# Sparse 3x3 convolution, float32 in and out: the last pair's load in two halves of 32 rows, the second one pair later

## Chip, cores, metric

One core of one Trainium2 chip. The metric is device microseconds (us) of one launch; the profile's span runs from the first to the last instruction and is some 1.8 us shorter. Executions come in a fast and, now and then, in a slow state some per cent longer; the kernel before was caught in it as well (128.5 to 131.5 us in five of its runs).

## The reference

```python
batch, c_in, h, w, c_out, k = 16, 64, 64, 64, 128, 3     # weight: 90% zeros
# x: (16, 64, 64, 64) float32, weight: (128, 64, 3, 3) float32
x_pad = np.pad(x, ((0, 0), (0, 0), (1, 1), (1, 1)))
output[b, co] += weight[co, ci, kh, kw] * x_pad[b, ci, kh:kh+h, kw:kw+w]   # over ci, kh, kw
```

16.8 MB of input are read and 33.55 MB of output are written, both float32 in HBM.

## The kernel before

Images are taken in 8 pairs: two images of 64 channels fill the 128 partitions. A GpSimd DMA loads each pair and casts it to bf16. Each pair has four blocks of 16 rows. For a block GpSimd adds neighbouring rows (tile `s`), TensorE runs 30 matmuls, ScalarE copies a shared product, and VectorE adds it to the two others into the output buffers `o`. The SP queue stores them. All pairs' inputs have a buffer of their own; outputs have seven buffers, two for a pair.

```python
xs = [x_pool.tile([128, H, W], BF16, name=f"x{p}") for p in range(NP)]      # NP = 8
...
def load(p, a=0, b=H):
    nc.gpsimd.dma_start(out=xs[p][:, a:b, :], in_=pair(p)[:, a:b, :])

EARLY, CUT = 4, 24
for p in range(1, EARLY):
    load(p)
load(EARLY, 0, CUT)
...                                        # weights are transposed; product(), direct(), twos()
for p in range(NP):
    o = [o_pool.tile([C_OUT, H, W], FP32, name="o") for _ in range(2)]
    last = p == NP - 1
    for blk in range(4):
        r0 = 16 * blk
        if BLOCKS[p][blk] == "T":
            twos(p, o, r0)                 # GpSimd add, matmuls, ScalarE copies, VectorE adds
            if p == 1 and blk == 3:
                load(EARLY, CUT, H)
            elif p > 1 and blk == 3 and p + EARLY - 1 < NP:
                load(p + EARLY - 1)        # pair 5 after pair 2, 6 after 3, 7 after 4
        ...
        if last and blk % 2 == 1:
            for n in range(2):
                rows = slice(r0 - 16, r0 + 16)
                nc.sync.dma_start(out=out[2 * p + n][:, rows, :], in_=o[n][:, rows, :])
    if not last:
        for n in range(2):
            nc.sync.dma_start(out=out[2 * p + n], in_=o[n])
```

## Time and profile before

| | before |
|---|---|
| median of the first three runs | 126.33 us (126.23 to 126.84) |
| span of the profiled run | 124.3 us |
| TensorE busy | 108.9 us (88%) |
| VectorE, ScalarE, GpSimd busy | 82.2, 39.0, 41.1 us |
| HBM read and written | 17.07 and 33.55 MB |
| last VectorE add ends / last store packet ends | 112.0 / 123.0 us |

How to read it: an engine's busy share is an average over stages, and the DMA engines are not among the engines of the first table. Read the strip of 40 slices by column: while the DMA row shows 9 in every slice, it hardly matters how full the others are. The queues q0 (loads issued by GpSimd, with cast) and q1 (SP: stores, weights and the first half pair) run on the same 16 DMA engines. The GB/s of the page count a casting load by the bf16 that it writes, half of what it reads; rates that I call HBM rates count loads twice. How long loads take to land is in the page's table of DMA issues (KB by the bf16 side, us from issue to landing):

```profile
x<-in_x_dram POOLq DMA_DIRECT2D x6, 1024.0 KB, 15.7
```

### The profile page before, as it was taken

How to read it: one execution, taken by the hardware profiler on the slowest of the kernel's cores; microseconds unless marked ns; L12 is line 12 of the kernel's file. 1: busy time of each engine (PE TensorE's matmuls, PEld its weight loads, DVE VectorE, ACT ScalarE, POOL GpSimd, SP SyncE). 2: the span in 40 equal slices, each digit the busy share in tenths (PEclk: the TensorE clock that was granted, in tenths of full speed). 3: DMA queues.
4: the chain of work that ended last, by engine and by line, in shares of the span. 5: the costliest groups of instructions: out<-in, count | busy, mean ns of one | idle time of the engine just before them, and what ended most of it. 6: DMA issues, size and time to landing. Idle time of an engine off the chain costs nothing.

```text
span 124.3 us, 2549 instructions
## 1 busy us (share of the span) xinstructions
PE 108.9 (88%) x1030; PEld 59.8 (48%) x1030; DVE 82.2 (66%) x135; ACT 39.0 (31%) x71; POOL 41.1 (33%) x46
## 2 busy tenths in 40 slices
PE   6989999999999999999999999999999999960000
PEld 6845555555555555555555555555555555520000
DVE  0354677877787778777877787778888788870000
ACT  4545323333333333333333333333333333310000
POOL 6428253533353335333533333343333310000000
PEclk9999999999999999999999999999999999998555
DMA  4999999999999999999999999999999999999991
GB/s 130 348 225 216 214 219 213 203 418 311 346 409 411 316 298 327 432 319 329 308 422 332 308 306 409 432 432 430 427 438 416 438 427 432 422 419 414 424 409 82
DMA packets 4196, 42.93 MB, mean 345 GB/s; under 512 B 472, under 2 KB 472, under 8 KB 984
## 3 DMA queue, kind: packets, MB, share of 16 engines
q1 hardware_dynamic: 2888, 34.90, 66.8%
q0 software_dynamic: 1296, 7.86, 30.8%
q8 instruction: 8, 0.13, 0.4%
q14 instruction: 4, 0.03, 0.1%
HBM read 17.07 MB, written 33.55 MB: 407 GB/s over the span
## 4 chain that ended last, share of the span: by engine, by line
PE 82%; DMA 5%; DVE 1%; issue 1%; DVEq 0%; SPq 0%
PE ps L148 82%; DMA o<-in_x_dram 5%; DVE o L181 1%; DVEq L240 0%; DVE x L99 0%; SPq L60 0%; DVEq L181 0%
## 5 line engine op out<-in xcount | busy, mean ns | idle before, releaser
L181 DVE TENSOR_TENSOR o<-ps,pc 128x512 f32<-128x512 f32 x124 | 77.7, 685 | 22.2 <-PE ps L148 19.8
L148 PE MATMUL ps<-x,wT 64*128 64x504 bf16 (+3 forms) x780 | 88.8, 373 | 0.6 <-DVE x L99 0.6
L148 PEld LDWEIGHTS <-wT 64*128 64x128 bf16 x966 | 54.8, 94 | 48.9 <-issue 0.6
L167 POOL TENSOR_TENSOR s<-x 128x512 bf16<-128x512 bf16 x31 | 35.5, 1149 | 57.6 <-PE ps L148 40.2
L174 ACT COPY pc<-ps 128x512 f32<-128x512 f32 x62 | 33.3, 590 | 64.0 <-issue 61.8
L148 PE MATMUL ps<-s,wT 64*128 64x512 bf16 (+1 forms) x186 | 25.7, 377 | 0.0
L84 PE MATMUL ps<-idle_rhs 128*128 128x128 bf16 x55 | 4.8, 265 | 1.0 <-DVE idle_rhs L79 1.0
L84 PEld LDWEIGHTS <-idle_rhs 128*128 128x128 bf16 x55 | 4.4, 122 | 1.0 <-DVE idle_rhs L79 1.0
L68 POOL DMA_DIRECT2D x<-in_x_dram x8 | 4.4, 559 | 0.0
L103 DVE CAST w_bf<-w_sb 128x192 bf16<-128x192 f32 (+1 forms) x4 | 1.1, 345 | 2.7 <-DMA w_sb<-in_weight_dram 2.7
L162 DVE COPY o<-ps 128x512 f32<-128x512 f32 x2 | 1.4, 692 | 2.0 <-PE ps L148 2.0
L161 ACT COPY o<-ps 128x512 f32<-128x512 f32 x2 | 1.2, 586 | 2.4 <-PE ps L148 2.4
L99 ACT CAST x<-o 128x576 bf16<-128x576 f32 (+1 forms) x2 | 1.5, 802 | 1.1 <-DMA o<-in_x_dram 1.1
L99 DVE CAST x<-o 128x576 bf16<-128x576 f32 x1 | 0.5, 459 | 2.1 <-DMA o<-in_x_dram 2.1
L103 ACT ACT_TABLE_LOAD x1 | 1.3, 1283 | 0.7 <-PEq L229 0.7
L103 ACT CAST w_bf<-w_sb 128x64 bf16<-128x64 f32 (+1 forms) x2 | 0.7, 416 | 1.6 <-DMA w_sb<-in_weight_dram 1.6
L109 PE MATMUL ps<-ident,w_bf 128*128 128x128 bf16 x9 | 1.0, 276 | 0.1
L113 DVE TENSOR_TENSOR wT<-ps,wT 128x384 bf16<-128x384 f32 x2 | 1.0, 546 | 0.0
L109 PEld LDWEIGHTS <-w_bf 128*128 128x128 bf16 x9 | 0.7, 120 | 0.5 <-DVE w_bf L103 0.5
L63 POOL DMA_DIRECT2D x<-in_x_dram x1 | 0.7, 693 | 0.8 <-POOLq L229 0.8
L79 DVE MEMSET idle_rhs<- 128x64 uint32 x1 | 0.1, 112 | 0.8 <-PEq L229 0.8
L122 ACT CAST wT<-ps 128x384 bf16<-128x384 f32 x1 | 0.5, 478 | 0.4 <-PE ps L109 0.4
(8 smaller groups left out, 1.9 us busy)
## 6 DMA issues: line engine op xcount, KB each, us to landing
out_dram<-o SPq DMA_DIRECT2D x14, 2048.0 KB, 17.9
x<-in_x_dram POOLq DMA_DIRECT2D x6, 1024.0 KB, 15.7
out_dram<-o SPq DMA_DIRECT2D x4, 1024.0 KB, 12.0
o<-in_x_dram SPq DMA_DIRECT2D x1, 1024.0 KB
x<-in_x_dram POOLq DMA_DIRECT2D x1, 640.0 KB, 14.3
x<-in_x_dram POOLq DMA_DIRECT2D x1, 512.0 KB, 7.6
x<-in_x_dram POOLq DMA_DIRECT2D x1, 384.0 KB, 25.2
w_sb<-in_weight_dram SPq DMA_DIRECT2D x1, 288.0 KB
```

What stands on the lines that cost most here:

```text
L68: nc.gpsimd.dma_start(out=xs[p][:, a:b, :], in_=pair(p)[:, a:b, :])
L84: nc.tensor.matmul(idle_ps, idle_rhs, idle_rhs, start=True, stop=True)
L99: copy(out=xs[0][:, a:b, :], in_=x_head[:, a:b, :])
L103: copy(out=w_bf4[:, g, a:b, :], in_=w_v[:, k : k + b - a, :])
L109: nc.tensor.matmul(wps[:, j, :], src, ident, start=True, stop=True)
L113: nc.vector.tensor_tensor(out=wT[:, g], in0=wps, in1=wT[:, G1], op=SUB)
L148: nc.tensor.matmul(ps[n][:, lo:hi, c_lo:c_hi], tap(g, kw, n), src[q, a:b:step, c_lo + kw - 1 : c_hi + kw - 1], start=(i == 0), stop=(i == ...
L161: nc.scalar.copy(out=o[0][:, r0 : r0 + rows, :], in_=ps[0])
L162: nc.vector.tensor_copy(out=o[1][:, r0 : r0 + rows, :], in_=ps[1])
L167: nc.gpsimd.tensor_tensor(out=s, in0=xs[p][:, r0 : r0 + 16 : 2, :], in1=xs[p][:, r0 + 1 : r0 + 16 : 2, :], op=ADD)
L174: nc.scalar.copy(out=c, in_=shared[n])
L181: nc.vector.tensor_tensor(out=o[n][:, first : r0 + 16 : 2, :], in0=ps[n], in1=pc[n], op=ADD)
```

## The change

The intent: make room for stores where the last load stood, and let its second half come one pair later.

```diff
     EARLY, CUT = 4, 24
+
+    LATER = {2: (5,), 3: (6,), 4: (7, 0, 32), 5: (7, 32, 64)}
     for p in range(1, EARLY):
         load(p)
     load(EARLY, 0, CUT)
@@
                 if p == 1 and blk == 3:
                     load(EARLY, CUT, H)
-                elif p > 1 and blk == 3 and p + EARLY - 1 < NP:
-                    load(p + EARLY - 1)
+                elif blk == 3 and p in LATER:
+                    load(*LATER[p])
```

## The prediction

> **What bounds the kernel now.** I read the page's strip of 40 slices first, then its DMA lines, then the chain of waits, then windows of the late part, and last the GpSimd timeline, because the change moves a GpSimd load. From the page:
>
> ```profile
> span 124.3 us, 2549 instructions
> PE   6989999999999999999999999999999999960000
> DMA  4999999999999999999999999999999999999991
> ...
> q1 hardware_dynamic: 2888, 34.90, 66.8%
> q0 software_dynamic: 1296, 7.86, 30.8%
> ...
> HBM read 17.07 MB, written 33.55 MB: 407 GB/s over the span
> ```
>
> TensorE is full until slice 36 and then has nothing to do for the last tenth of the span, while the DMA row is at 9 from slice 2 to slice 39. The two queues (q1 stores, q0 the casting loads) together take 66.8 + 30.8 = 97.6% of the 16 engines' time. The loads count half in the GB/s row, as that counts the bf16 that is written; by HBM bytes it is 17.07 + 33.55 = 50.62 MB. The chain of waits, in order of time, ends earlier than the program does:
>
> ```profile
> 7.38 102.09 PE ps L148 x954
> ...
> 111.42 0.60 DVE o L181
> ```
>
> It follows TensorE for 102 us and stops at 112.02 us, where the last VectorE add ends. The other 12.3 us are the stores draining, which this view does not follow. Windows show the late part (columns: us, busy time of PE, PEld, DVE, ACT, POOL with counts, granted clock, DMA share, GB/s):
>
> ```profile
> 76.00:80.00 4.00, 4.00 (x42) 2.06 (x38) 3.22 (x6) 1.72 (x4) 1.33 (x2) 1.00 1.03 438
> 80.00:84.00 4.00, 4.00 (x40) 2.13 (x38) 2.59 (x5) 1.50 (x3) 2.13 (x2) 1.00 0.98 416
> 84.00:88.00 4.00, 4.00 (x42) 2.15 (x38) 3.41 (x6) 1.07 (x2) 1.15 (x1) 1.00 1.01 430
> ...
> 112.00:116.00 4.00, 0.00 (x0) 0.00 (x0) 0.02 (x1) 0.00 (x0) 0.00 (x0) 0.76 1.00 422
> 116.00:120.00 4.00, 0.00 (x0) 0.00 (x0) 0.00 (x0) 0.00 (x0) 0.00 (x0) 0.50 1.01 428
> 120.00:121.00 1.00, 0.00 (x0) 0.00 (x0) 0.00 (x0) 0.00 (x0) 0.00 (x0) 0.50 0.93 393
> 121.00:122.00 1.00, 0.00 (x0) 0.00 (x0) 0.00 (x0) 0.00 (x0) 0.00 (x0) 0.50 0.60 254
> 122.00:123.00 1.00, 0.00 (x0) 0.00 (x0) 0.00 (x0) 0.00 (x0) 0.00 (x0) 0.50 0.16 66
> ```
>
> The reader is to see that stores alone run at about 428 GB/s (mean of 438, 416, 430) with a DMA share of 1, that this goes on after the compute has ended, and that only the last 2 to 3 us taper off, as the 16 engines do not finish together. 50.62 MB / 428 GB/s = 118.3 us of pure transfer inside a span of 124.3; what remains is the first few us, the taper and the final completion. So the bound is the total of DMA bytes. TensorE comes close behind it: in the drain window (112 to 124.3) 4.11 MB still move, of which the last two stores, issued at 111.45 and 112.04, are 2.10 MB. So 2.0 MB, 4.7 us at 428 GB/s, were already queued ahead of them: TensorE could end some 4.7 us later before the DMA engines ran dry.
>
> **What the Trainium skill says.** "DMA: Bandwidth & Descriptors", section "Issuing engines are not separate DMA queues", says that DMAs from any issuing engine end up on the same 16 DMA engines and interleave. The trace agrees: while load and stores overlap, from 62 to 77 us, the queue shares are 34.8% and 66.5%, 101% in sum. The same page, section "Where 436 GB/s comes from", gives 435 GB/s as the ceiling of a core's SBUF ports; it also says that HBM binds at about 358 GB/s. The trace agrees with the first (428 in steady state) and not with the second, so I use 428. The same page, section "Queues, rings and completion order", says each DMA engine goes round robin between its queues by packets. The trace agrees in kind: a load beside queued stores lands after 15.7 us (median), where 2.1 MB of HBM alone would take 4.9 us.
>
> **The change, part by part.** It leaves pairs 5 and 6 (loads at the ends of pairs 2 and 3) as they are. The load of pair 7, one issue of 64 rows after the last block of pair 4, becomes 32 rows there and 32 rows after the last block of pair 5. GpSimd's timeline of before gives the moments:
>
> ```profile
> 60.25 1.15 POOL L167 TENSOR_TENSOR s<-x 128x512 bf16<-128x512 bf16 x1 [2.01 <-PE ps L148]
> 61.34 0.57 POOL L68 DMA_DIRECT2D x<-in_x_dram  x1
> ...
> 73.05 1.15 POOL L167 TENSOR_TENSOR s<-x 128x512 bf16<-128x512 bf16 x1 [2.01 <-PE ps L148]
> 76.20 1.15 POOL L167 TENSOR_TENSOR s<-x 128x512 bf16<-128x512 bf16 x1 [2.00 <-issue]
> ...
> 95.50 1.16 POOL L167 TENSOR_TENSOR s<-x 128x512 bf16<-128x512 bf16 x1 [2.09 <-PE ps L148]
> 98.67 1.15 POOL L167 TENSOR_TENSOR s<-x 128x512 bf16<-128x512 bf16 x1 [2.01 <-PE ps L148]
> ```
>
> Counting four adds to a pair back from the last, 98.67 is the last block of pair 7, 73.05 that of pair 5 and 60.25 that of pair 4.
>
> 1. Bytes: none added, none removed. The 1.05 MB (HBM side) of the second half go from 61 to 77 us to the stretch after 74 us. Both stretches are full, so the stores take over what is freed, 1.05 MB / 428 = 2.5 us earlier at most, and give it back in the second stretch. Effect on the end: 0.
> 2. GpSimd: one more issue of 0.56 us (the median of the eight), at about 74.1, in an idle stretch of 2.0 us before the add at 76.20. Off the path: 0.
> 3. Packets: 128 more data packets and 16 more 4-byte ones, as a load has 144 packets (1296 in nine loads). In the DMA records of the trace a load packet that reads 16 KB takes 0.624 us and one that reads 8 KB 0.324: two halves are 0.024 us dearer. 128 pairs x 0.024 / 16 engines = 0.19 us, and 16 x 0.02 / 16 = 0.02 us: +0.21. The store packets give less: 0.309 for 8 KB against 0.611 for 16 KB, 0.007 a pair, so 8 x 0.007 = 0.06 us. The 8 KB load packets ran beside the start's other loads, which flatters the difference, so I take +0.1 us.
> 4. Deadline of the second half. Each engine has eight load packets. In before these eight 16 KB packets, beside stores, took from about 62 to 76 us: 14 us, or 1.75 us a turn, of which 0.62 is the load packet and about 1.1 are stores. With 8 KB packets a turn is 1.1 + 0.32 = 1.45 us, and eight are 11.6 us; with 1.5 us of issue and completion the half lands at about 74.1 + 13 = 87. GpSimd first reads it for the third block of pair 7, at 95.50: 8 us in hand. TensorE reads row 32 in the odd rows of the second block, at about 102.9 by its timeline. Nobody waits: 0.
>
> Sum: 126.33 + 0.1 = 126.4 us.
>
> **The rivals.**
>
> *A: the second half lands late and stalls TensorE.* For it: a load has taken up to 25.2 us to land (the one at the start, queued behind the others); 25 us from 74.1 is 99.3, after the add at 95.50. Against it: beside stores the loads took 14.3 to 15.7 us, and this is half of one. Even at 99.3 the add would have to be done only before TensorE wants its result at 104.08 (the third block of pair 7), and an end of TensorE up to 4.7 us later is still hidden by the queued stores. Time if it came true in this form: 126.4 to 126.9. To cost 2% (2.5 us) the stall would have to pass 7 us.
>
> *B: the stores that go earlier free an output buffer sooner, and the kernel gains.* There are seven output buffers for two per pair, so the second output of pair 6 reuses that of the first store of pair 3, which landed at 79.5, some 6 us before pair 6 writes. That is the tightest I find. But no wait of VectorE on an output store is in the list of waits:
>
> ```profile
> DVE o L181 <- PE ps L148: 19.8, 27, 1.3
> DVE o L181 <- ACT pc L174: 2.3, 4, 0.6
> ```
>
> These are the only waits of the add: the matmuls and the ScalarE copy. A buffer freed sooner releases nobody. Gain: 0.
>
> *C: the stores run dry for a moment because the load has left their stretch, and the DMA engines idle.* By 73 us five pairs' outputs, 21 MB, are about to be queued and the stores' queue has moved some 13.3 MB, so over 7 MB wait, 17 us of work; taking 1.05 MB from this leaves over 6 MB. Cost: 0.
>
> *D: the order of packets changes how unevenly the engines finish.* The taper from 120 to 123 us moves (0.93 + 0.60 + 0.16) = 1.7 us worth of full work in 3 us, so 1.3 us are lost to unevenness. I can't tell from the profile which engine is late or why. If the change shifts it, it is by some tenths either way: 126.0 to 126.8.
>
> **Range and chances.** The centre is 126.4. The three runs before already span 126.23 to 126.84, so the noise is about 0.6; D adds some tenths either way, A and the packet cost only upward. Range for 8 in 10: 125.9 to 127.0. Faster by over 2% means under 123.8, which is less than the present end of transfers allows: everything lost at both ends is about 124.3 - 118.3 = 6 us, and the change touches none of it; chance 0.02. Slower by over 2% means above 128.9, which needs A far beyond any landing seen, or a loss in mixing the queues that no stretch of before shows; chance 0.03. Within 2%: 0.95.
>
> **What would show it right or wrong.** Right: the strip's DMA row at 9 as before; q0 with 1440 packets and the same 7.86 MB; one more load issue near 74 us; half loads landing 11 to 15 us after issue; no GpSimd wait on a load after the first 20 us; windows at 420 to 438 GB/s from 88 us; the last add at 112 us; the span within 0.5 us of 124.3. Step 4 is wrong if the list of waits shows adds or matmuls waiting for the load of pair 7 after 90 us, and step 1 is wrong if a window between 61 and 90 us has a DMA share well below 1. A taper shorter or longer than 3 us with all else equal would be D. A time below 124 or above 129 would mean that the DMA bound itself is misread.

## The result

126.31 us median against 126.31 us, six runs each. The ratio of the fast runs is 0.9988, with a 95% interval of 0.9965 to 1.001: the same time. (A ratio is the mean time of one kernel's fast runs over that of the other's fast runs in the same rounds, so it is not quite the ratio of the medians.) One of the six runs of the changed kernel was slow, 131.61 us. Such runs came with the kernel before too, so nothing is read from it.

The page of the changed kernel, the lines that answer to those of before:

```profile
span 124.2 us, 2550 instructions
...
DMA  4999999999999999999999999999999999999992
...
q1 hardware_dynamic: 2888, 34.90, 67.0%
q0 software_dynamic: 1440, 7.86, 30.9%
...
x<-in_x_dram POOLq DMA_DIRECT2D x3, 512.0 KB, 13.7
```

One instruction and 144 packets more, the same bytes, the same full DMA row. (Three loads are of 512 KB: the two halves of pair 7 and the half of pair 0 at the start.) The chain of waits still ends with the last VectorE add at 112.1 us, while the stores run on:

```profile
7.51 102.04 PE ps L150 x954
...
111.49 0.60 DVE o L183
```

GpSimd's timeline has the new issue where it was expected, and no add of pair 7 comes late:

```profile
73.12 1.15 POOL L169 TENSOR_TENSOR s<-x 128x512 bf16<-128x512 bf16 x1 [2.01 <-PE ps L150]
74.22 0.57 POOL L68 DMA_DIRECT2D x<-in_x_dram  x1
76.29 1.14 POOL L169 TENSOR_TENSOR s<-x 128x512 bf16<-128x512 bf16 x1 [1.50 <-issue]
...
95.56 1.15 POOL L169 TENSOR_TENSOR s<-x 128x512 bf16<-128x512 bf16 x1 [2.08 <-issue]
```

What did move is the order of the bytes. In windows of the changed kernel (same columns as before) the GB/s of 72 to 76 us is 417 where it was 342, because half a load is gone from there and stores have its place; from 80 to 88 us it is the other way round (416 and 430 before, in the prediction; 357 and 389 now). First the line of before, then those of the changed kernel:

```profile
72.00:76.00 4.00, 4.00 (x42) 2.16 (x38) 3.41 (x6) 1.08 (x2) 1.15 (x1) 1.00 1.00 342
```

```profile
72.00:76.00 4.00, 4.00 (x42) 1.86 (x40) 3.42 (x6) 1.07 (x2) 1.66 (x2) 1.00 1.02 417
...
80.00:84.00 4.00, 4.00 (x40) 1.82 (x38) 2.55 (x6) 1.57 (x4) 1.83 (x2) 1.00 1.05 357
84.00:88.00 4.00, 4.00 (x42) 1.89 (x40) 3.41 (x6) 1.07 (x2) 1.15 (x1) 1.00 1.00 389
...
120.00:121.00 1.00, 0.00 (x0) 0.00 (x0) 0.00 (x0) 0.00 (x0) 0.00 (x0) 0.50 0.97 410
```

The DMA share, second from the right, is 0.97 or more in each of these. The first store of pair 3 landed at 76.8 us instead of 79.5, so the stores do run 2.7 us ahead for a while, and by the last ones nothing of it is left: the first of the last four landed at 115.9 against 116.1, and the last packet ended at 122.9 against 123.0.

### The profile page after: what moved, and what is told of

Same layout as the page of the kernel before. It is cut to its first block, busy times and chain, and to the rows that moved or that the text cites. A ratio compares the mean times of both kernels' runs of the same rounds, so it can differ in the third digit from the quotient of the medians.

```text
span 124.2 us, 2550 instructions
## 1 busy us (share of the span) xinstructions
PE 109.7 (88%) x1030; PEld 52.9 (43%) x1030; DVE 82.2 (66%) x135; ACT 38.9 (31%) x71; POOL 41.6 (34%) x47
## 4 chain that ended last, share of the span: by engine, by line
PE 85%; DMA 2%; DVE 1%; issue 1%; DVEq 0%
PE ps L150 82%; DMA w_sb<-in_weight_dram 2%; PE ps L86 2%; DVE o L183 1%; PE ps L111 1%; DVEq L242 0%; DVE w_bf L105 0%; DVEq L183 0%
## 5 line engine op out<-in xcount | busy, mean ns | idle before, releaser
L150 PEld LDWEIGHTS <-wT 64*128 64x128 bf16 x966 | 47.1, 94 | 55.8
L150 PE MATMUL ps<-s,wT 64*128 64x512 bf16 (+1 forms) x186 | 25.2, 377 | 0.0
L86 PE MATMUL ps<-idle_rhs 128*128 128x128 bf16 x55 | 5.4, 287 | 1.0 <-DVE idle_rhs L81 1.0
L86 PEld LDWEIGHTS <-idle_rhs 128*128 128x128 bf16 x55 | 5.1, 136 | 1.0 <-DVE idle_rhs L81 1.0
L68 POOL DMA_DIRECT2D x<-in_x_dram x9 | 5.0, 560 | 0.0
L63 POOL DMA_DIRECT2D x<-in_x_dram x1 | 0.7, 693 | 0.8 <-POOLq L231 0.8
```

Of the source, the lines that this page charges most:

```text
L86: nc.tensor.matmul(idle_ps, idle_rhs, idle_rhs, start=True, stop=True)
L150: nc.tensor.matmul(ps[n][:, lo:hi, c_lo:c_hi], tap(g, kw, n), src[q, a:b:step, c_lo + kw - 1 : c_hi + kw - 1], start=(i == 0), stop=(i == ...
```

## Experiments

The theory: the end is set by the total of DMA bytes, at about 428 GB/s of HBM traffic with no gap; TensorE runs a little ahead of that bound, so the order of loads matters only where it makes the DMA engines idle. The rivals: the compute sets the end; loads among the stores cost something of their own; each packet costs something of its own. Eleven kernels, all of them variants of the changed one, were run. Two of them compute wrong results on purpose. Each ratio is to the kernel before, run in the same rounds, which takes the same time as the changed one. The medians are of all runs, the ratios of the fast ones alone; one run each of the kernels without pair 7's load, with quarters and with short packets was slow. A trace is of one execution, the times are of four to six.

### The split alone

```diff
-    LATER = {2: (5,), 3: (6,), 4: (7, 0, 32), 5: (7, 32, 64)}
+    LATER = {2: [(5,)], 3: [(6,)], 4: [(7, 0, 32), (7, 32, 64)]}
-                    load(*LATER[p])
+                    for piece in LATER[p]:
+                        load(*piece)
```

> The split alone: both halves of pair 7's load are issued after the last block of pair 4. Theory (the total of DMA bytes sets the end, and neither packet count nor order of loads matters at this size): same time as before, 126.3, within 0.3 us; both halves land by about 78 us. Rival (each load packet costs a fixed 0.024 us of engine time, 8 more data packets on each engine): +0.2 us, which 5 rounds may just show.

Measured: 126.17 us, ratio 0.9997 (0.9966 to 1.0028). Same. The halves landed at 75.3 and 82.9 us, the second later than the 78 that I expected: the halves go one after the other, and each takes some 7.6 us beside stores (more on this below). The interval is too wide to tell 0 from 0.2 us.

### The delay alone

```diff
-    LATER = {2: (5,), 3: (6,), 4: (7, 0, 32), 5: (7, 32, 64)}
+    LATER = {2: (5,), 3: (6,), 5: (7,)}
```

> The delay alone: pair 7's load whole, one pair later, issued near 74.2 us. It should land near 74.2 + 15.8 = 90 us, about 1 us after GpSimd's first add of pair 7 was due (89.1), but 7 us before TensorE wants that sum (97.7). Theory (DMA bound, compute has slack): one short GpSimd wait on the load of about 1 us, no TensorE wait, time 126.3 within 0.3. Rival (a late load stalls the compute and shows in the end): +1 us or more.

Measured: 126.31 us, ratio 0.9992 (0.9962 to 1.0022). The load landed at 89.9 us. The list of waits from 85 to 112 us has one wait of GpSimd on it, an idle stretch of 2.9 us, of which about 2 us are the usual gap between adds; TensorE waits for nothing there:

```profile
POOL s L169 <- DMA x<-in_x_dram: 2.9, 1, 2.9
```

### The second half two pairs later

```diff
-    LATER = {2: (5,), 3: (6,), 4: (7, 0, 32), 5: (7, 32, 64)}
+    LATER = {2: (5,), 3: (6,), 4: (7, 0, 32), 6: (7, 32, 64)}
```

> The second half two pairs later instead of one, issued near 87.1 us. It should land near 87.1 + 13.7 = 101 us, 5 us after GpSimd's add of pair 7's third block was due (95.6), but 1 to 2 us before TensorE reads row 32 (102.9) and 3 us before it wants the third block's sum (104.1). Theory: GpSimd waits about 5 us, TensorE under 0.5 us, time 126.3 within 0.3. Rival (GpSimd's adds are close to the path): + 3 to 5 us.

Measured: 126.32 us, ratio 0.9989 (0.9959 to 1.0019). The half landed at 100.7 us, and GpSimd's add came 5.3 us late. TensorE did not wait in this window, as the adds are made well ahead of it:

```profile
POOL s L169 <- DMA x<-in_x_dram: 7.4, 1, 7.4
```

So the half of the changed kernel could come a further pair later and still cost nothing that these runs can show (0.3% either way).

### The whole load two pairs later

```diff
-    LATER = {2: (5,), 3: (6,), 4: (7, 0, 32), 5: (7, 32, 64)}
+    LATER = {2: (5,), 3: (6,), 6: (7,)}
```

> Pair 7's load whole and two pairs later, issued near 87.1, landing near 103; TensorE wants the first block's sum of pair 7 at 97.7, so it stalls about 103 + 1.2 - 97.7 = 6.5 us and the last stores are issued near 118.5 instead of 112. Theory (about 4.7 us of stores are queued ahead of the last two, less some start-up of a store): the queue runs dry for about 2 to 4 us and the time becomes 128 to 130. Rival (TensorE's end sets the time one to one): 132.8. Rival (bytes alone count): 126.3.

Measured: 130.91 us (129.96 to 131.35), ratio 1.0339 (1.029 to 1.0389), some 4.3 us more: above my range of 128 to 130. Here TensorE does wait, and the DMA engines do run dry (waits, then windows):

```profile
PE ps L150 <- POOL s L169: 7.7, 1, 7.7
```

```profile
104.00:112.00 8.00, 6.48 (x37) 2.82 (x38) 1.75 (x3) 1.07 (x2) 4.45 (x4) 0.57 1.00 428
112.00:114.00 2.00, 2.00 (x22) 1.03 (x20) 1.27 (x3) 1.07 (x2) 0.00 (x0) 1.00 0.10 41
114.00:116.00 2.00, 2.00 (x22) 1.02 (x20) 2.00 (x4) 0.53 (x2) 0.00 (x0) 1.00 0.04 8
```

The stall was 7.7 us, not 6.5. It also cost TensorE part of its clock: the clock records show a granted clock of 0.5 from 100.7 to 110.9 us, so that TensorE, back at work at 105.52, ran 5.4 us at half speed and lost another 2.7 us (the 0.57 above, third from the right, is a mean over the 8 us). 7.7 + 2.7 = 10.4 us, which is just how late the last store was issued (122.55 instead of 112.12). "TensorE: Matmul & The Clock Gate", section "What's actually happening", in the Trainium skill says that the clock falls to half after an idle window of about 3.4 us and comes back after as long a busy one, and that these windows run freely, whenever the work starts. The trace agrees in kind: the clock fell 2.9 us after the last matmul (97.78 to 100.70) and came back 5.4 us after the first one.

What the delay costs can be read from the DMA share. From 112 to 116 us alone it leaves 2 x 0.90 + 2 x 0.96 = 3.7 us idle. The sum over all packets (their HBM bytes at 428 GB/s against the time that passed) says that from 88 us to the last packet this run lost 6.3 us and the changed kernel 1.1, the taper included. Of the 5.2 us between them 0.6 come from a dip to 311 GB/s at 91 to 94 us, as the load began, and 4.5 from the time after 100 us, when stores were missing. The span is 129.2 against 124.2. That lost DMA time and longer span agree is bookkeeping, as both kernels move the same bytes. What the run shows is that 10.4 us of delay left the DMA engines idle for only about 4.5 us (4.3 us of time in the mean of the runs): about 6 us were absorbed (4.7 predicted). The time is near that of slow runs (131.6 us), but apart from the dip this trace has the usual 405 to 432 GB/s from 88 to 112 us.

### Pair 7 not loaded (wrong result on purpose)

```diff
-    xs = [x_pool.tile([128, H, W], BF16, name=f"x{p}") for p in range(NP)]
+    xs = [x_pool.tile([128, H, W], BF16, name=f"x{p}") for p in range(NP - 1)]
+    xs.append(xs[-1])
-    LATER = {2: (5,), 3: (6,), 4: (7, 0, 32), 5: (7, 32, 64)}
+    LATER = {2: (5,), 3: (6,)}
```

> Wrong result on purpose: pair 7 is never loaded, its outputs are computed from pair 6's input, with the same instructions on every compute engine. 2.10 MB of HBM reads fewer. Theory (DMA bytes set the end): 2.10 MB / 428 GB/s = 4.9 us less, at most; since TensorE still ends near 110 and the last two stores then find nearly nothing queued ahead, 1 to 2.5 us of that may be lost: 121.5 to 124. Rival (compute sets the end): 126.3 unchanged.

Measured: 124.23 us, ratio 0.9832 (0.9816 to 0.9848). The time falls by 0.0168 x 126.4 = 2.1 us with the compute unchanged (last add at 112.0 us). It does not fall by 4.9, because the queue now runs dry before pair 6's stores come at 98.6 us:

```profile
96.00:98.00 2.00, 2.00 (x23) 1.12 (x20) 1.27 (x4) 0.49 (x2) 0.67 (x1) 1.00 0.50 213
98.00:100.00 2.00, 2.00 (x23) 1.06 (x20) 1.42 (x4) 1.07 (x2) 1.15 (x1) 1.00 0.33 139
```

2 x 0.50 + 2 x 0.67 = 2.3 us idle; 4.9 - 2.3 = 2.6, near the 2.1 measured. This shows both that DMA bytes set the end of the kernel and how near the compute is behind: with 2.1 MB less the stores have to wait for it at 96 to 100 us.

### A third fewer matmuls in pairs 6 and 7 (wrong result on purpose)

```diff
+    fewer = []
-        todo = [(t, kw) for t in terms for kw in KW_ORDER]
+        todo = [(t, kw) for t in terms for kw in (KW_ORDER[:2] if fewer else KW_ORDER)]
...
+        if p == NP - 2:
+            fewer.append(1)
```

> Wrong result on purpose: in pairs 6 and 7 one of the three kernel columns is left out, a third fewer matmuls there; DMA as in the changed kernel. TensorE's work of 25.5 us for the two pairs falls to about 17, but VectorE needs 11 us a pair, so the last add should end some 3 us earlier, near 109. Theory (DMA bytes set the end): time 126.3 within 0.3. Rival (compute sets the end): 2.5 to 3.5 us less.

Measured: 125.94 us, ratio 0.9984 (0.9956 to 1.0011): no difference clear of the noise. The last add ended at 105.8 us, even 6 us earlier than in the changed kernel (I expected 3). Of those 6 us nothing clear of noise arrived at the end. The DMA share goes on at 1 without any compute beside it:

```profile
104.00:112.00 8.00, 0.00 (x0) 0.00 (x0) 1.75 (x3) 0.00 (x0) 0.00 (x0) 0.66 0.99 423
```

So the compute does not set the end.

### Loads of pairs 5, 6 and 7 in quarters

```diff
-    LATER = {2: (5,), 3: (6,), 4: (7, 0, 32), 5: (7, 32, 64)}
+    LATER = {p: [(p + 3, a, a + 16) for a in (0, 16, 32, 48)] for p in (2, 3, 4)}
```

(with the loop over pieces of the first experiment)

> Loads of pairs 5, 6 and 7 each as four issues of 16 rows, at the places of before: 9 more issues, 1152 more data packets, 72 more on each engine. Rival that the prediction's term of packets rests on (each load packet has 0.024 us of its own in the records: 6, 8, 10 and 16 KB packets take 0.248, 0.324, 0.398 and 0.624 us): 72 x 0.024 = 1.7 us more, 128.0. Theory (these fixed parts overlap in the engines: the DMA share is 1.03 while loads run alone at the same 428 GB/s): same, 126.3 within 0.3. GpSimd gets 1.7 us more to issue at each of three places, in idle time.

Measured: 127.74 us (126.68 to 128.93), ratio 1.0099 (1.0056 to 1.0142). My theory's "same" was wrong here, and the reason is one that neither side had named. From the second piece of pair 5 on, the pieces landed one after the other some 5 to 6 us apart (53, 59, 65, 71, 77, 82, 88, ... us), the last at 111.8 us. GpSimd waited for them, and in the end TensorE too, 3.3 us in all. The list of waits, and a window in which the DMA engines ran partly dry:

```profile
POOL s L169 <- DMA x<-in_x_dram: 23.5, 5, 5.0
```

```profile
116.00:118.00 2.00, 0.46 (x6) 0.02 (x2) 1.82 (x4) 0.00 (x0) 0.00 (x0) 1.00 0.72 303
```

The last store was issued at 117.85 instead of 112.12. The DMA packets show why: from 40.3 to 110.8 us, while these pieces were under way, 1536 load packets went beside some 1430 store packets, about one for one, though a store packet is four times as large as a piece's (16 KB against 4 KB read). The packed trace doesn't name the engine of a packet, so that the engines take them in turn is inferred from these counts. A load has 8 packets for each engine, so a quarter takes 8 x (0.61 of a store packet + 0.17) = 6.2 us; the half of the changed kernel took 8.2. Small loads get a smaller share of the bytes. The HBM rate from 40 to 104 us, from the queues' MB, is (20.81 + 2 x 3.07) / 64 = 421 GB/s against (20.96 + 2 x 3.15) / 64 = 426 in the changed kernel: 0.8 us lost over 72 packets more on each engine, 0.011 us each where my own reading of the packet durations had said 0.024. The late data costs as well: the share of 0.72 above leaves 0.56 us idle, where the changed kernel has none. By its HBM bytes this run was 1.3 us behind the changed kernel at 120 us, and made up 0.5 us of that in a shorter taper (422 to 425 GB/s up to 123 us). But it is the fastest of the six, only 0.6 us above the profiled run of the changed kernel; how the 1.3 us of the mean divide is not shown.

### Short packets at the start, without stores

```diff
     for p in range(1, EARLY):
-        load(p)
+        for h in range(2):
+            nc.gpsimd.dma_start(
+                out=xs[p].rearrange("q (a b r) w -> q a b r w", a=2, b=2)[:, :, h],
+                in_=pair(p).rearrange("q (a b r) w -> q a b r w", a=2, b=2)[:, :, h],
+            )
```

> Packet cost by itself: the loads of pairs 1 to 3, which run at the start with no store beside them, are cut into runs of 16 rows (two issues a pair, each of two separate runs of 16 rows on every partition): 72 more data packets on each engine, as in the run with quarters, but early and in good time. If each packet's own part counts in full (0.024 us): the load of pair 3 lands 1.7 us later than in the changed kernel (24.2 there) and the time is 128.0. If it counts as the windows of the run with quarters say (427 against 421 GB/s over 64 us, 0.9 us for 72 packets, 0.012 us each): 0.9 us later, time 127.1. If the parts overlap wholly: 24.2 and 126.3.

Measured: 127.55 us, ratio 1.0079 (1.0049 to 1.0109), 1.0 us more. That fits the middle expectation in size, but not in place. Windows of this kernel, and then of the changed one:

```profile
8.00:12.00 4.00, 4.00 (x42) 2.14 (x38) 1.99 (x5) 1.54 (x3) 3.31 (x3) 1.00 1.03 163
12.00:24.00 12.00, 12.00 (x116) 6.36 (x112) 8.65 (x15) 4.53 (x9) 5.20 (x6) 1.00 1.12 211
```

```profile
8.00:12.00 4.00, 4.00 (x42) 1.85 (x38) 1.79 (x4) 1.37 (x3) 3.37 (x3) 1.00 1.06 223
12.00:24.00 12.00, 12.00 (x116) 5.48 (x114) 8.65 (x15) 4.34 (x9) 5.09 (x5) 1.00 1.02 209
```

From 12 to 24 us the short packets move about as many GB/s as the long ones (211 against 209), with a DMA share of 1.12: most of what each packet has of its own overlaps in the engines. Not all of it: counted in HBM bytes, and only from 12 to 20 us, before the cut load of pair 4 and the first stores mix in, it is 418 GB/s against 426 to 430 in five kernels with long packets, or 0.2 us for 38 packets more on each engine, 0.005 us each. Most of the loss, (223 - 163) / 223 x 4 = 1.1 us by these lines (0.8 us by HBM bytes, 335 against 425 GB/s), is in the 4 us in which the loads of pairs 1 to 3 begin. Why they begin slowly there (more issues on GpSimd, the last at 6.76 us instead of 4.05; or the short packets themselves) stays open.

### All loads at the start

```diff
-    LATER = {2: (5,), 3: (6,), 4: (7, 0, 32), 5: (7, 32, 64)}
+    LATER = {}
     load(EARLY, 0, CUT)
+    load(EARLY, CUT, H)
+    for p in range(EARLY + 1, NP):
+        load(p)
```

(and the load in the loop after pair 1 removed)

> The opposite order: all loads issued at the start, no load among the stores. Loads share the engines with stores until near 50 us, stores land later, and an output buffer of pair 3 may come free about 1 us late. Theory (order of loads does not matter, the total of bytes does): time 126.3 within 0.4, possibly a VectorE wait of 1 to 3 us on a store near 48 us that is hidden by the end. Rival (loads among the stores are needed for the time): 2 us or more on top.

Measured: 127.59 us, ratio 1.0094 (1.0077 to 1.0111), 1.2 us more; my expectation of 0.4 at most was wrong. No VectorE wait on a store appeared. The packets show an HBM rate of 296 GB/s from 24 to 28 us, 400 in the changed kernel. The first store, issued at 22.5, moved its first packet only at 27.1 us (issued at 21.9 and moved at 24.6 in the changed kernel), and in between the load packets were slow. The dip is worth (400 - 296) / 428 x 4 = 1.0 us, most of the 1.2.

### All loads at the start, pair 4 not cut

```diff
-    load(EARLY, 0, CUT)
-    load(EARLY, CUT, H)
-    for p in range(EARLY + 1, NP):
+    for p in range(EARLY, NP):
         load(p)
```

(against the run above)

> All loads at the start as in the run before, but pair 4's load not cut into 24 and 40 rows. In that run the DMA records show 296 GB/s in the stretch 24 to 28 us, with 6 KB and 10 KB load packets taking 0.43 and 0.55 us instead of 0.25 and 0.40, just before the first store moves. If the cut load is the cause: the dip goes, and the time falls from 127.6 to 126.4. If the start of the stores behind a long queue of loads is the cause: the dip and about 127.5 stay.

Measured: 127.02 us, ratio 1.004 (1.0007 to 1.0072). The dip stays (341 GB/s from 24 to 28 us; at 24 us load packets that read 16 KB took 1.05 us instead of 0.62), so the cut is not its whole cause. It is smaller than in the run above, and so is the time: both expectations missed in part. The dip goes with the start of the stores behind queued loads; that this is its cause is not shown, and why load packets slow down then, I can't tell from these traces.

### Pair 4's load whole at the start, the rest as changed

```diff
-    load(EARLY, 0, CUT)
+    load(EARLY)
-                if p == 1 and blk == 3:
-                    load(EARLY, CUT, H)
-                elif blk == 3 and p in LATER:
+                if blk == 3 and p in LATER:
```

> A candidate to beat both kernels: the changed kernel with pair 4's load whole at the start, one DMA fewer. Both kernels lose about 0.5 us at 20 to 28 us, where 6 KB load packets run (411 and 394 GB/s against 428). If the short packets are the cause: up to 0.4 us less, 125.9; if the start of the stores is the cause: 126.3, same.

Measured: 126.6 us, ratio 1.001 (0.9981 to 1.0039): no gain. The dip is there too (346 GB/s from 24 to 28 us). No version beats the two kernels by more than the noise.

## Why the prediction was right

The time (126.31 against 126.4 predicted, range 125.9 to 127.0) held. By its steps:

- **The bound.** Shown from three sides. Fewer bytes made it faster with the compute unchanged (2.1 us), less compute did not (0.2 us, within noise), and a compute that ended 10.4 us later cost only about 4.5 us, the time for which stores were missing. What holds the rate at 428 GB/s (the engines, the ports or HBM), no run here separates.
- **Step 1, bytes moved and none saved.** Held: the stores ran 2.7 us ahead (2.5 at most was estimated) and gave it back.
- **Step 2, GpSimd's issue.** Held: 0.57 us at 74.22, with the next add at 76.29 instead of 76.20.
- **Step 3, packets, +0.1 us.** Too small to be seen in the time of this change. Its basis, 0.024 us of each packet, was mis-sized: alone, short packets cost about 0.005 us each in steady flow, and beside stores 0.011 us; for the 8 packets more on each engine that is 0.1 us or less. The reason given for taking less, that the 8 KB packets at the start were flattered, did not hold: beside stores they took 0.322 us, as against 0.324.
- **Step 4, the landing at 87 us.** It was 87.9, but through two errors that cancelled. I had let the load's packets begin soon after the issue, with two store packets to each load packet. In fact nothing of the load moves at first. The queues of the changed kernel, from 74.8 to 78.6 us and from 78.6 to 88 us (packets, MB, share of the 16 engines):

```profile
q1 hardware_dynamic: 107, 1.62, 99.9%
```

```profile
q1 hardware_dynamic: 205, 2.92, 74.1%
q0 software_dynamic: 144, 0.52, 27.6%
```

  For 4.5 us after the issue stores alone move; then the half's 128 data packets take 8.2 us beside 132 store packets, about one for one: 8 x (0.61 + 0.32) = 7.4 us. The remaining 1.0 us lies between the last packet and the landing. What I had taken for the first packets of pair 7's load in the kernel before, near 62 us, were the last of pair 6's load.
- **Rival A, late data.** Its mechanism is real but far off: the half could be a pair later still at no cost, and the whole load two pairs later did what the rival says. The figure for what is absorbed was 4.7 us; the run with the whole load two pairs later showed about 6.
- **Rival B, an earlier free buffer.** No VectorE wait on a store appears in either list.
- **Rival C, the stores run dry.** Not in the change; shown where pair 7 was not loaded, at 96 to 100 us.
- **Rival D, the taper.** 0.97 + 0.64 + 0.14 = 1.75 us of full work in the last 3 us of transfers, against 1.69 before: unchanged. What makes the engines finish unevenly stays open. In the two kernels whose queue ran dry between 112 and 118 us (the whole load two pairs later, and the quarters) it was shorter: 0.2 and 0.5 us lost, against 1.0 in the changed kernel.

## What to carry to other kernels

When the DMA engines are full from end to end, moving a transfer only reorders bytes; look for bytes to save or for idle DMA time, and price a delay of the compute by the DMA idle time that it makes. Before moving a load later, work out its landing from the delay before its first packet plus its packets per engine times one packet of each queue that shares the engines; cutting a load into pieces makes each piece smaller but not quicker in proportion (beside stores the packets of a whole, a half and a quarter took 10.3, 8.2 and about 6 us here). And a number that comes out right is not proof of its working: the landing here was right by two errors that cancelled.

## What the Trainium skill lacked or had wrong

- "DMA: Bandwidth & Descriptors", section "Latency and other measured facts", gives about 1 us to the first byte of a load issued by GpSimd. Here it was 4.1 us for the first load of the program (issued at 1.24, first packet at 5.35) and 4.2 to 5.1 us for loads beside stores (74.22 to 78.70 in the changed kernel). For stores it gives about 0.6 us: 0.8 us here with idle DMA engines (115.50 to 116.33), but 2.5 to 4.6 us for the first store behind queued loads.
- The same page, section "Queues, rings and completion order", says that an engine drains a packet of typically 9 to 17 descriptors before it turns to the next queue. Here 128 load records of a half went beside 132 store records of 16 KB, and those of a whole load beside 121 to 152, so that the queues seem to take turns record by record and a load of 8 records on each engine takes 8 turns: quarters of a pair landed some 6 us apart beside stores, where their bytes alone need 1.2 us at 428 GB/s. The page does not spell out that a smaller load gets a smaller share.
- The same page, section "Where 436 GB/s comes from", has HBM bind at about 358 GB/s in transfers between HBM and SBUF; one core alone moved about 428 GB/s to and from HBM for most of 120 us. This is a fault of that sentence and not of the page, whose section "Measured (HBM→SBUF, 128 partitions, SWDGE, issued from GpSimd)" has 425 GB/s for 16 MB and one core alone, and 358 for each of two that stream together.
- No page that I read has the dip when the first stores start behind queued loads: 394 to 400 GB/s over 4 us in the two kernels, 296 to 346 with longer queues of loads.
